# Stores of the split weights issued by ScalarE and GpSimd instead of SyncE

## The chip, the cores and the metric

The kernel runs on one core of one Trainium2 chip. The metric is the device time of one execution in microseconds; the kernel before took 3095.43 us, the median of three runs (3093.91 to 3096.95). Five engines work side by side on a core: TensorE (PE in the profile, with PEld for its weight loads), VectorE (DVE), ScalarE (ACT), GpSimd (POOL) and SyncE (SP), which computes nothing and in this kernel issues nearly all DMAs. Each engine takes its instructions in order and waits at one until its semaphores allow it.

## The reference, cut to what matters

The program computes one layer of a streaming encoder for 2048 frames of 1024 channels, in float32:

```
h = rmsnorm(x) * (1 + scale) + shift
q_lat, kv_lat, k_rope, gm_in, rw_in, z, g = split(h @ w_in)      # 7712 columns
y_mla = attention, block-causal, 8 heads; q and k,v from q_lat, kv_lat by w_uq, w_ukv
y_gm  = u * (W_s layernorm(v) + b)                               # 128-frame blocks
y_rw  = RWKV-7 recurrence: state = state * decay + ..., 8 heads of 64
merged = sum_n (y_n * silu(z_n)) @ w_br[n] * sigmoid(g_n)
out = x + gate * rmsnorm(merged @ w_out)
```

What counts here is that all 2048 frames are multiplied by the same weights `w_in`, `w_br`, `w_out`, `w_uq` and `w_ukv`, a block of frames at a time.

## The kernel before, in words

The frames are worked on in four super-blocks of 512. Within each come the projections of `w_in`, the recurrence (`wkv`), and the attention (`attention`), during which the next super-block's projections and the finishing work of the previous one fill TensorE's free time.

A product is made to near float32 accuracy from two rounded parts of each operand, a high part (the value rounded to TensorE's fast float32 format) and a low part (the rest): `mm3` multiplies high by high, high by low and low by high. A projection (`gemm`) of 128 output channels for 512 frames takes 24 such matmuls of 128 by 512, in two groups of four 128-row pieces of the weight.

`wgran` (line 558) delivers the two parts of one group's weight, 128 by 512 values, 256 KB each. When the group is asked for the first time, it loads the raw weight into a buffer `wr`, ScalarE rounds it into `wh` (the high part), and VectorE or GpSimd subtracts to make `wl` (the low part), whichever has the smaller modelled backlog (`split`, line 534). Then `keep` (line 544) stores both parts in DRAM tensors named `kept`. Every later super-block loads them from there (`again`, line 550). So the stores are issued once for each group of each weight: for `w_in` in the first super-block, for `w_br` and `w_out` a little later, up to some 1120 us. The attention's up-projection weights go the same way in tiles `wuq`, `wuqh`, `wuql` of half the size (`weights`, twelve groups). There are three buffers each of `wr`, `wh` and `wl`, and two each of `wuq`, `wuqh`, `wuql`; a buffer can be written again when all that reads it has ended, the store among them. The first super-block's output gates are projections whose 256 KB result (`gt`) is stored as well (`gate_d`).

In the recurrence each pair of heads (`hp`, four in all) makes a small triangular inverse on VectorE (`X`, `tx`), which goes to DRAM in four stores (`xd`) and comes back in another arrangement in eight loads (`xtb`) before TensorE can go on with the chain of that pair. GpSimd takes part in that chain with small operations (`el`, `bkb`, `r`, `rkb`, `m21`, `dg`, and the two operations of a reciprocal root).

The order of TensorE's instructions is written out ahead of time by a planner, `Pace`. It keeps a modelled clock: `note` (line 143) gives each instruction a duration and a place on its engine, `ready` tells when a thread of work can go on, and `run` takes the thread to be stepped next. For a DMA the clock takes 0.45 us on one place called "queue", 1.1 us of latency, the bytes' time on one place called "DMA", and 0.8 us until it is landed. The order of the other engines' instructions, SyncE's included, follows from a scheduler of the language; loads of weights are given a higher priority there, so they stand ahead of other work in SyncE's order.

Of the kernel before, what the change touches and what calls it, by code (L numbers as in the profile page):

```python
# [11 lines left out]
F32 = mybir.dt.float32  # L12
# [78 lines left out]
class Pace:  # L91
# [55 lines left out]
    def note(self, i):  # L147
        eng = str(i.engine).split(".")[-1]
        dma = "DMA" in type(i).__name__
        src, dst, n, full, f32 = [], [], 1, 0, False  # L150
        for l, aps in ((src, i.ins), (dst, i.outs)):
            for a in aps:
                ap = getattr(a, "bass_ap", None)
                if ap is None:
                    continue
                l.append(ap.tensor.name)
                m = 1
                for _, c in a.ap[1:]:
                    m *= c
                full += l is src and m > 1  # L160
                if dma:
                    m = 4 * m * a.ap[0][1]
                if eng != "PE" or l is dst:
                    n = max(n, m)
                elif a.dtype == F32:
                    f32 = True
        dep = 0.0
        for x in src:
            dep = max(dep, self.after(self.wrote.get(x), eng))
        for x in dst:  # L170
            for e in self.used.get(x, {}).items():
                if not (dma and e[0] == "DMA"):
                    dep = max(dep, self.after(e, eng))
        if eng == "PE":
            nr, nc = i.tile_size
            dur = n * (4 if f32 and not i.is_transpose else 2 if f32 else 1) / 2400 * nr * nc / P ** 2
            t = self.t = max(self.t, dep) + dur
            self.pe += dur
        elif dma:
            dur = n / 3.6e5  # L180
            t = self.slot("queue", max(dep, self.t - self.early), .45) + 1.1
            t = self.slot("DMA", t, dur) + dur + DLAT
            eng = "DMA"
        else:
            psum = any(x.startswith(("pd", "ps")) for x in src)
            op = type(i).__name__
            if eng == "Activation":
                f = str(i.func).split(".")[-1]
                if f in ("Exp", "Gelu", "Sin") and f != self.table or f == "Tanh" and self.table not in ("Exp", "Gelu"):
                    self.table = "Exp" if f == "Tanh" else f  # L190
                    t = self.slot(eng, max(dep, self.t - self.early), 1.28)
                dur = .05 + n * .00084 + .04 * (not psum) + .09 * (len(src) > 1) + .09 * (len(dst) > 1)
            elif eng == "DVE":
                dur = .065 + n / (960 if psum or full > 1 or n < 128 else 1920) + .065 * (full < len(src))
                if "Reciprocal" in op:
                    dur = .07 + n * .0063
                elif "Scan" in op or "Reduce" in op:
                    dur = n * (.0021 if "Scan" in op else .00118)
            else:
                dur = .12 + n * .00216 if n <= 512 else .55 + n * .0013  # L200
                if n <= 16 and "TensorTensor" in op:
                    dur = .3 + n * .165
            dur *= SLOW
            t = self.slot(eng, max(dep, self.t - self.early), dur) + dur
        for x in dst:

            self.wrote[x] = (eng, max(t, self.wrote[x][1]) if dma and x in self.wrote else t)
        for x in src + dst:
            u = self.used.setdefault(x, {})
            u[eng] = max(u.get(eng, 0.0), t)  # L210
# [96 lines left out]
def trunk(ctx, tc, io, out):  # L307
    nc = tc.nc
    pace = Pace()
    V, A, G, PE, SY = (pace.engine(e) for e in (nc.vector, nc.scalar, nc.gpsimd, nc.tensor, nc.sync))  # L310
# [231 lines left out]
    kept = {}  # L542

    def keep(key, h, l):

        kept[key] = [dr.tile(list(x.shape), F32, name="kept") for x in (h, l)]
        for d, x in zip(kept[key], (h, l)):
            SY.dma_start(d, x.bitcast(F32))

    def again(key, h, l):  # L550

# [6 lines left out]
    def wgran(key, fill):  # L558

        if key in kept:  # L560
            tags = [("wr", "wh"), ("wl", "wr"), ("wh", "wl")][turns[0] % 3]
            turns[0] += 1
            h, l = (wp.tile([P, 4, P], F32R, tag=g, name="wh" if n == 0 else "wl", bufs=WHB) for n, g in enumerate(tags))
            again(key, h, l)
            return h, l
        raw = wp.tile([P, 4, P], F32, tag="wr", name="wr", bufs=WRB)
        with tc.high_priority(offset=100):
            fill(raw)
        h = wp.tile([P, 4, P], F32R, tag="wh", name="wh", bufs=WHB)
        l = wp.tile([P, 4, P], F32R, tag="wl", name="wl", bufs=WHB)  # L570
        split(h, l, raw)
        keep(key, h, l)
        return h, l
# [159 lines left out]
    def mla_units(s, pl):  # L733
# [14 lines left out]
        def weights(key, fill):  # L748
            hl = wparts()
            if key in kept:  # L750
                again(key, *hl)
                return hl
            w = pl.tile([P, 2, P], F32, tag="wuq", name="wuq", bufs=2)
            fill(w)
            parts(w, *hl)
            keep(key, *hl)
            return hl
# [999 lines left out]
```

## Time and profile before

| What | us |
|---|---|
| median of three runs (lowest, highest) | 3095.43 (3093.91, 3096.95) |
| the profiled execution: its time | 3098.93 |
| its span, first to last instruction | 3096.6 |
| mean granted TensorE clock, share of full speed | 0.97 |

A page of the profile gives the busy time of each engine and its share of the span; the views behind it tell, for any stretch, what each engine waited for and what ended the wait. A row of a timeline reads: start in us from the span's start, duration in us, engine, line, operation, out<-in, shapes, count, and in brackets the engine's idle time before it with what ended that. All instructions bear line 120, a helper that records them, so one reads by the tiles' names. An engine's name with a q (SPq, ACTq) marks the sequencer's own instructions, such as the issue of a DMA, which are not counted as busy.

### The profile page before, as it was taken

What the parts mean: (1) busy time and instruction counts of PE and PEld (TensorE: products, weight loads), DVE (VectorE), ACT (ScalarE), POOL (GpSimd) and SP (SyncE); (2) the same over time, 40 slices, a digit from 0 to 9 for tenths busy, and PEclk for the clock granted to TensorE, in tenths of its full rate; (3) what the DMA queues carried; (4) which work ended last, traced back from release to release, by engine and by line L of the source; (5) the groups of instructions that cost most, each with busy time, mean ns of one, the idle gap of its engine ahead of it and who ended that gap; (6) DMA issues with size and microseconds to landing.
All of it is one profiled execution on the core that took longest, in us unless ns stands there. A gap on an engine that the chain in (4) does not pass through costs nothing.

```text
span 3096.6 us, 49478 instructions
## 1 busy us (share of the span) xinstructions
PE 2877.7 (93%) x16924; PEld 2330.6 (75%) x16924; DVE 1714.8 (55%) x4574; ACT 1235.2 (40%) x2868; POOL 598.8 (19%) x606
## 2 busy tenths in 40 slices
PE   5889988989989999999999998998899999899998
PEld 4667766777867777878877777887787677788886
DVE  6426675466257753466357653446645765356653
ACT  4325433444233433444333323454433333267641
POOL 3122232332021211131011101113100110222210
PEclk8999999989999999999999999999999999999999
DMA  7888755877766689765665578655557556844456
GB/s 270 260 273 252 223 176 164 268 237 244 231 211 196 198 252 286 223 203 173 211 210 174 167 236 266 201 164 187 160 168 243 179 158 215 263 143 134 124 183 218
DMA packets 521383, 645.84 MB, mean 209 GB/s; under 512 B 142160, under 2 KB 254892, under 8 KB 521132
## 3 DMA queue, kind: packets, MB, share of 16 engines
q1 hardware_dynamic: 520960, 642.64, 66.0%
q8 instruction: 134, 2.20, 0.3%
q14 instruction: 117, 0.96, 0.1%
q10 hardware_dynamic: 172, 0.05, 0.0%
HBM read 457.69 MB, written 184.81 MB: 207 GB/s over the span
## 4 chain that ended last, share of the span: by engine, by line
PE 59%; DVE 5%; DMA 4%; ACT 2%; issue 1%; POOL 1%; SPq 1%; POOLq 0%; DVEq 0%; ACTq 0%
PE pd L120 36%; PE pss L120 10%; PE pst L120 9%; PE pso L120 4%; DMA x<-in_x 1%; SPq L120 1%; DVE X L120 1%; DVE tx L120 0%; DMA tg<-gate_d 0%; DMA wr<-in_w_out 0%; DMA wl<-kept 0%; DMA yo<-yo_d 0%; ACT Y L120 0%; DMA xtb<-xd 0%; DMA wh<-kept 0%
## 5 line engine op out<-in xcount | busy, mean ns | idle before, releaser
L120 PE MATMUL pd<-hh,wh 128*128 128x512 f32 x1952 | 810.6, 415 | 16.7 <-ACT wh L120 6.4
L120 PE MATMUL pd<-hh,wl 128*128 128x512 f32 x1952 | 775.2, 397 | 7.8 <-POOL wl L120 5.9
L120 PE MATMUL pd<-hl,wh 128*128 128x512 f32 x1952 | 773.9, 396 | 2.8 <-DVE hl L120 1.8
L120 PEld LDWEIGHTS pd<-hh,wh 128*128 128x128 f32 x1952 | 373.3, 191 | 105.5 <-issue 13.2
L120 PEld LDWEIGHTS pd<-hh,wl 128*128 128x128 f32 x1952 | 372.2, 191 | 95.6 <-POOL wl L120 9.7
L120 PEld LDWEIGHTS pd<-hl,wh 128*128 128x128 f32 x1952 | 374.5, 192 | 71.1 <-DVE hl L120 3.6
L120 DVE TENSOR_TENSOR pw<-pst,ph 128x512 fp32r<-128x512 f32 (+2 forms) x352 | 196.3, 568 | 248.9 <-ACT ph L120 247.5
L120 ACT ACTIVATE ph<-pst 128x512 fp32r<-128x512 f32 (+2 forms) x352 | 171.5, 497 | 247.6 <-PE pst L120 211.2
L120 PE MATMUL pd<-brh,wh 128*128 128x512 f32 x576 | 252.3, 438 | 18.8 <-DVE gt L120 9.0
L120 PE MATMUL pd<-brh,wl 128*128 128x512 f32 x576 | 229.8, 399 | 0.6 <-POOL wl L120 0.6
L120 PE MATMUL pd<-brl,wh 128*128 128x512 f32 x576 | 230.2, 400 | 0.0
L120 DVE TENSOR_SCALAR_CACHE_REDUCE p<-pss 128x512 f32<-128x512 f32 (+2 forms) x320 | 191.2, 607 | 69.2 <-PE pss L120 65.2
L120 ACT ACTIVATE p<-p,nm 128x512 f32<-128x512 f32 (+3 forms) x288 | 189.7, 660 | 82.8 <-DVE nm L120 82.4
L120 POOL TENSOR_TENSOR wl<-wr,wh 128x512 fp32r<-128x512 f32 x98 | 131.2, 1341 | 435.4 <-ACT wh L120 347.5
L120 ACT ACTIVATE wh<-wr 128x512 fp32r<-128x512 f32 x162 | 101.1, 628 | 230.3 <-PE pd L120 89.0
L120 PE MATMUL pst<-consts,p 128*128 128x128 f32 x1088 | 162.4, 274 | 10.7 <-DVE za L120 5.8
L120 PE MATMUL pso<-ph,v 128*128 128x256 f32 x576 | 152.8, 288 | 0.0
L120 PEld LDWEIGHTS pd<-brh,wh 128*128 128x128 f32 x576 | 111.2, 193 | 52.3 <-issue 13.8
L120 PEld LDWEIGHTS pst<-consts,p 128*128 128x128 f32 x1088 | 128.8, 141 | 27.3 <-issue 12.0
L120 PE MATMUL pso<-pw,v 128*128 128x256 f32 x576 | 146.4, 283 | 1.2 <-DVE pw L120 1.2
L120 PE MATMUL pss<-kh,qh 96*128 96x512 f32 (+2 forms) x320 | 129.3, 404 | 18.2 <-ACT kh L120 15.2
L120 POOL TENSOR_TENSOR kl<-stg,kh 96x512 fp32r<-96x512 f32 x80 | 103.4, 1296 | 220.5 <-ACT kh L120 214.2
(295 smaller groups left out, 4820.7 us busy)
## 6 DMA issues: line engine op xcount, KB each, us to landing
wh<-kept SPq DMA_DIRECT2D x486, 256.0 KB
wl<-kept SPq DMA_DIRECT2D x486, 256.0 KB
kept<-wh SPq DMA_DIRECT2D x162, 256.0 KB
kept<-wl SPq DMA_DIRECT2D x162, 256.0 KB
wr<-in_w_in SPq DMA_DIRECT2D x120, 256.0 KB
gate_d<-gt SPq DMA_DIRECT2D x64, 256.0 KB
part_d<-gt SPq DMA_DIRECT2D x64, 256.0 KB
p<-part_d SPq DMA_DIRECT2D x64, 256.0 KB
```

Of the source, the lines that this page charges most:

```text
L120: r = f(*a, **k)
```

## The change

`keep` gives the store of the high part to ScalarE's queue (`A`) and that of the low part to GpSimd's (`G`); before, SyncE (`SY`) issued both. `keep` is called by `wgran` and by `weights`, for each group once. In the planner's clock a DMA's place on "queue" becomes a place on the queue of the engine that issues it. Buffers, tensors and bytes stay as they are, and so do the loads in `again`.

```diff
@@ -178,7 +178,7 @@
             self.pe += dur
         elif dma:
             dur = n / 3.6e5
-            t = self.slot("queue", max(dep, self.t - self.early), .45) + 1.1
+            t = self.slot("queue of " + eng, max(dep, self.t - self.early), .45) + 1.1
             t = self.slot("DMA", t, dur) + dur + DLAT
             eng = "DMA"
         else:
@@ -544,8 +544,8 @@
     def keep(key, h, l):
 
         kept[key] = [dr.tile(list(x.shape), F32, name="kept") for x in (h, l)]
-        for d, x in zip(kept[key], (h, l)):
-            SY.dma_start(d, x.bitcast(F32))
+        for e, d, x in zip((A, G), kept[key], (h, l)):
+            e.dma_start(d, x.bitcast(F32))
 
     def again(key, h, l):
```

## Rows read from the trace of the kernel before

**Rows 1.** The page: busy us of each engine, share of span, instructions.

```profile
PE 2877.7 (93%) x16924; PEld 2330.6 (75%) x16924; DVE 1714.8 (55%) x4574; ACT 1235.2 (40%) x2868; POOL 598.8 (19%) x606
```

**Rows 2.** Stretches: length, busy PE PEld DVE ACT POOL, clock, DMA share, GB/s.

```profile
0.00:30.00 30.00, 8.05 (x34) 5.45 (x34) 14.05 (x24) 16.45 (x33) 2.00 (x7) 1.00 0.91 334
88.00:126.00 38.00, 27.42 (x91) 19.48 (x90) 27.54 (x41) 10.16 (x20) 5.61 (x12) 0.82 0.81 248
130.00:242.00 112.00, 95.32 (x417) 74.18 (x418) 28.63 (x48) 32.22 (x52) 25.01 (x25) 0.97 0.84 271
242.00:640.00 398.00, 366.71 (x2334) 286.95 (x2334) 247.72 (x662) 172.88 (x369) 121.28 (x105) 0.95 0.70 218
```

**Rows 3.** Waits of PE, 126 to 242 us: total us, times, longest us.

```profile
PE pd L120 <- ACT wh L120: 6.4, 4, 2.3
PE pd L120 <- POOL wl L120: 3.6, 6, 0.9
...
PE pd L120 <- DVE wl L120: 1.6, 1, 1.6
```

**Rows 4.** Group, 130 to 242 us: busy, mean ns | idle before, what ended it.

```profile
L120 ACT ACTIVATE wh<-wr 128x512 fp32r<-128x512 f32 x30 | 18.9, 631 | 60.8 <-DMA kept<-wh 34.0 <-DMA kept<-wl 9.8 <-PE pd L120 6.0
```

**Rows 5.** ACT's timeline, 190 to 212 us.

```profile
192.97 0.63 ACT L120 ACTIVATE wh<-wr 128x512 fp32r<-128x512 f32 x1 [2.04 <-PE pd L120]
...
207.09 0.63 ACT L120 ACTIVATE wh<-wr 128x512 fp32r<-128x512 f32 x1 [0.72 <-DMA kept<-wh]
```

**Rows 6.** SP's timeline, 160 to 240 us.

```profile
203.15 0.38 SPq L120 DMA_DIRECT2D wr<-in_w_in  x1
203.59 0.50 SPq L120 DMA_DIRECT2D kept<-wh  x1
...
216.02 0.38 SPq L120 DMA_DIRECT2D wr<-in_w_in  x1
```

**Rows 7.** POOL's timeline, 190 to 212 us.

```profile
201.84 1.28 POOL L120 TENSOR_TENSOR wl<-wr,wh 128x512 fp32r<-128x512 f32 x1 [9.54 <-ACT wh L120]
```

**Rows 8.** PE's timeline, 198 to 204 us: first and last of 15 matmuls.

```profile
197.76 0.39 PE L120 MATMUL pd<-hh,wh 128*128 128x512 f32 x1
...
200.93 0.39 PE L120 MATMUL pd<-hh,wl 128*128 128x512 f32 x1
```

**Rows 9.** The tile kept, whole span, then 242 to 640 us: ns min/median/max, starts.

```profile
L120 SPq DMA_DIRECT2D kept<-wh x162: 319/446/1825, 35.0 to 1117.7; - x162
...
L120 SPq DMA_DIRECT2D kept<-wh x87: 319/444/1044, 243.1 to 638.7; - x87
```

**Rows 10.** Waits of PE, 88 to 126 us.

```profile
PE pst L120 <- DVE wuql L120: 4.2, 3, 1.9
PE pst L120 <- ACT wuqh L120: 4.0, 3, 2.1
```

**Rows 11.** SP's timeline, 90 to 96 and 460 to 470 us.

```profile
91.92 0.34 SPq L120 DMA_DIRECT2D kept<-wuql  x1
...
93.28 0.44 SPq L120 DMA_DIRECT2D wuq<-in_mla_w_uq  x1
...
462.13 0.50 SPq L120 DMA_DIRECT2D kept<-wh  x1
...
463.33 3.89 SPq L120 DMA_DIRECT2D xtb<-xd  x8
```

**Rows 12.** Waits of PE, 242 to 640 us.

```profile
PE pss L120 <- DMA xtb<-xd: 12.7, 5, 7.1
```

**Rows 13.** POOL's timeline, 284 to 316 us.

```profile
310.44 2.31 POOL L120 TENSOR_TENSOR bkb<-bk,E 128x1024 f32<-128x1024 f32 x1 [3.12 <-DMA xd<-X]
312.71 1.72 POOL L120 TENSOR_TENSOR wl<-wr,wh 128x512 fp32r<-128x512 f32 x1
```

**Rows 14.** ACT's timeline, 0 to 12 us: first and last of 11 loads.

```profile
4.68 0.25 ACTq L120 DMA_DIRECT2D rows<-in_rw_k_k  x1
...
11.12 0.30 ACTq L120 DMA_DIRECT2D rows<-in_b_ada  x1
```

## The prediction, made before the changed kernel ran

> **What bounds the kernel now.** I read the page first. TensorE is busy 2877.7 of 3096.6 us [rows 1], so at most 219 us are idle in the whole kernel, and the change can only give back idle time, or slow matmuls, in the stretches where stores of the weights' parts are issued. The table of stretches [rows 2] comes next. From 130 to 242 us, where the first projections stream their weights in, TensorE is busy 95.3 of 112 us, the DMA engines have a share of 0.84, and the granted clock is 0.97. From 242 to 640 us (the first recurrence) TensorE is busy 366.7 of 398 us, ScalarE 172.9, GpSimd 121.3.
>
> What does TensorE wait for between 126 and 242 us? Three rows name the weights' parts: 6.4 us for the high part, 3.6 and 1.6 us for the low part, 11.6 us in all [rows 3]. And what holds those parts back? The high parts are written by ScalarE, and of the 60.8 us that ScalarE idles ahead of its 30 activations, 34.0 us end with a DMA store of a high part and 9.8 us with one of a low part [rows 4]. So the three buffers of a part come free too late: a new part can't be written until the part of three groups ago is stored.
>
> One buffer followed through the timelines shows why. A high part was written at 192.97 us (0.63 us) [rows 5]. Its store was issued at 203.59 us, ten microseconds later, right behind a weight load issued at 203.15 us [rows 6]. That load waited until GpSimd had finished the low part that it began at 201.84 us (1.28 us) [rows 7], because it refills the raw buffer which that operation reads. SyncE's queue is in order, so the finished part's store sat behind a load that could not go yet. The activation that needed the buffer ran at 207.09 us, released by a store [rows 5]. This is a loop: store, buffer, part, load, next store. It turns over four groups, two gate projections, in 12.9 us (loads at 203.15 and 216.02 us [rows 6]), 6.4 us each, while TensorE's 24 matmuls of a projection need 5.4 us: 15 starts lie between 197.76 and 200.93 us, 0.226 us apart [rows 8].
>
> **The change, part by part.** It moves 162 stores of high parts [rows 9] and as many of low parts off SyncE, and 12 and 12 smaller ones of the attention's up-projections: the high parts' to ScalarE, the low parts' to GpSimd. No byte is added or removed, and no tensor changes. Of what leaves SyncE I count:
>
> First, the loop above. A high part's store no longer stands behind a load; ScalarE issues it after its own activation. At stake are the 11.6 us of rows 3. What is late next is the DMA system: 112 us at 271 GB/s become 292 GB/s if 8 us go, and the highest rate of any stretch I read is 334 GB/s at a share of 0.91 [rows 2]. I take two thirds, 8 us, between 0 and 11.6. With a clock of 0.97 the stretch also loses 0.03 x 112 = 3.4 us to slow matmuls, some of it after waits of other causes; I take 1.5, between 0 and 3.4.
>
> Second, the attention's query weights, 88 to 126 us. TensorE waits 4.2 and 4.0 us for them [rows 10]. Their raw load at 93.28 us stands behind three stores of parts that start at 91.92 us [rows 11]: 1.36 us in each of about three rounds, 4.1 us at most. I take 3. The clock there is 0.82 [rows 2], worth 6.8 us in 38; I take 1 of it, since the waits shrink and do not vanish.
>
> Third, the recurrence's way through DRAM. Ahead of the eight loads at 463.33 us stand two stores from 462.13 us on [rows 11], 1.2 us; TensorE waited 12.7 us for these loads in five waits [rows 12]. Two of the four head pairs show long waits, so 2 us, between 0 and 2.4. Sum of gains: 8 + 1.5 + 3 + 1 + 2 = 15.5 us, from 0 to 11.6 + 3.4 + 4.1 + 3 + 2.4 = 24.5.
>
> What is added. ScalarE issues 174 stores. On SyncE such an issue has a median of 0.45 us [rows 9], so about 78 us over the stretch to 1120 us. In the recurrence it is 87 stores [rows 9], 39 us, a tenth of 398 us, so each of some 80 ScalarE steps (20 for each head pair) meets one with a chance of 0.1 and waits half of 0.45: 1.8 us, half of it where TensorE hangs on the chain, 1 us. Elsewhere the second PSUM bank of the projections hides it: ScalarE's evacuation may come 5.4 us late before TensorE stops.
>
> GpSimd issuing a store is not in this trace. From below its price is SyncE's shortest issue, 0.32 us [rows 9]; from above the long GpSimd operation in the same stretch, 2.31 us [rows 13]. I take 1.3, the length of GpSimd's operation on the very same tile [rows 7]. In the recurrence as many stores, 87 x 1.3 = 113 us, bring GpSimd from 121 to 234 of 398 us [rows 2]. The code has nine GpSimd steps for each head pair (el, bkb, r, rkb, m21, two dg, two for the rsqrt), 36 in all; each finds a store ahead with a chance of 113/398 = 0.28 and waits half of 1.3 us: 6.6 us, half of it felt by TensorE, 3.3. With 0.32 us it is 0.2, with 2.31 it is 11. A low part that VectorE made adds a wait on GpSimd: behind that store stand GpSimd's next low part or its next step of the chain, and TensorE waits for either. Such a collision is to be seen already: a low part began only at 312.71 us, when the operation of 2.31 us before it was done [rows 13].
>
> Here the Trainium skill speaks against the change. SBUF — State Buffer, "Who interferes with whom", says that descriptor generation by GpSimd is blocked while VectorE works in its 2-port modes, and advises issuing from ScalarE or SyncE instead. No row here shows a store issued by GpSimd; by the rule the price would lie toward the upper end, a loss of 11 instead of 3.3 us.
>
> Third cost: ScalarE may have to wait before it may issue at all. At the start ScalarE issues eleven small loads of 0.23 to 0.31 us between 4.68 and 11.42 us [rows 14]; they fill 3 of 6.7 us, and nothing of ScalarE lies between them. The other 3.8 us, 0.38 per issue, look like waits for earlier transfers, of SyncE's too. At 0.38 x 87 = 33 us in the recurrence, worked out like the issue time, that is 0.6 us; I take 2.5, since single waits can be long, from 0 to the third rival. Sum of costs 1 + 3.3 + 2.5 = 6.8.
>
> The other edit gives the ordering clock a queue for each engine. It alters only the order of TensorE's instructions and which of VectorE and GpSimd makes a low part: with two stores in three gone from the modelled SyncE queue, loads are thought to arrive a little earlier. Before, a projection's seven DMAs took 7 x 0.45 = 3.15 us of modelled queue against 5.1 us of matmuls, so that queue seldom decided. I put this at nothing, between -10 and +10 us, roughly the largest single wait that another order could make or undo (the waits for the DRAM round trip sum to 12.7 [rows 12]).
>
> Net: 6.8 - 15.5 = -8.7 us. The profiled execution took 3098.9 us (its span 3096.6 and 2.3 us around it), which becomes 3090; it lies 3.5 us above the median of the runs, so for the median 3095.4 - 8.7 = 3087 us.
>
> **The rivals.** (1) The stores were not what mattered, and nothing measurable changes: 3095. For it: the raw loads wait for the low parts whoever stores them [rows 6, 7], and the DMA engines already have a share of 0.84. Against it: the buffer's release by a store [rows 4, 5]. The skill has this rival as a rule: DMA: Bandwidth & Descriptors, "Issuing engines are not separate DMA queues", says that several issuing engines save only the issue time. By it the time would stay; the trace disagrees so far in that the ten microseconds were an in-order wait, not issue time.
>
> (2) GpSimd becomes the bound, so the kernel is slower. In a projection GpSimd makes about one of the two low parts (1.29 us) and issues two stores; above (5.4 - 1.29) / 2 = 2.05 us for a store it can't keep up with TensorE. At 2.31 us, the first gain (8 + 1.5) is gone, 11 us are lost in the recurrence, and 3.5 us on ScalarE: 3095.4 + 11 + 3.5 - 6 = about 3104. For it: the neighbour of 2.31 us; against: GpSimd is busy only 25 of 112 us now [rows 2].
>
> (3) ScalarE stands at its stores until the eight loads of a head pair have landed. Their issue alone takes 3.89 us [rows 11], and a store issued at 203.59 us released its buffer for 207.09 us [rows 5, 6], 3.5 us later; between 3.9 and 7.4 us I estimate 6. Four head pairs make 24 us, and TensorE pays them, since ScalarE empties its banks: 3095.4 + 24 - 15.5 + 4.3 = 3108. It decides once ScalarE waits over 5.4 us, a projection's length. For it: the spread of ScalarE's own issues [rows 14]; against: in the projections, earlier transfers have landed by the time a part is made.
>
> (4) The new order decides, in either direction, by more than the stores do: 3078 or 3105.
>
> **How the numbers follow.** Forecast 0.52, rival 1 0.18, rival 2 0.08, rival 3 0.12, rival 4 0.10, half on each side. What this kernel's measurement can tell from no change is about 0.2%, 6.2 us, so 3089 to 3102 counts as the same. The forecast's own range, from its bounds, is 3071 (all gains, no cost) to 3094 (gains as taken, GpSimd at its upper price), and about a tenth of its weight lies above 3089. Faster: 0.46 + 0.05; same: 0.06 + 0.18; slower: 0.08 + 0.12 + 0.05 = 0.25. The range 3064 to 3110 takes in the full gain with a lucky order and both slower mechanisms.
>
> **What would show it.** Right: high-part stores issued within 1 us of their activation; ScalarE's activations of high parts no longer released by stores [rows 4]; the waits for parts down from 11.6 to about 4 us [rows 3]; a DMA share near 0.9 from 130 to 242 us. GpSimd's store near 1.3 us, and its busy time in the recurrence near 234 us. Wrong: stores on ScalarE that start several microseconds after the activation; more waiting for GpSimd's steps or the DRAM round trip than now [rows 12]; a first stretch as long as before. A TensorE order with many moved instructions and a changed end of the recurrence would mean rival 4.

## The result, and the profile after

The changed kernel takes 3116.41 us (median of nine runs, 3102.78 to 3132.46); the kernel before took 3095.07 us beside it (nine runs, 3089.79 to 3101.14). The ratio is 1.0069, with an interval of 1.0048 to 1.0091: slower by some 21 us, where 3087 was forecast, and outside the range of 3064 to 3110. Ratios here and below are of the runs as a whole and can differ by 0.1% from the ratio of two medians. One execution of a later experiment (high parts alone, 3796 us) is a slow one and is left out of its ratio. The profiled execution of the changed kernel took 3107.66 us, with a span of 3105.7. It lies 8.7 us below the median, so the trace shows only 9 of the 21 us as a longer span.

The page first, then the stretches (length, busy us and instructions of each engine, clock, DMA share, GB/s), against rows 1 and 2:

```profile
PE 2867.2 (92%) x16924; PEld 2327.4 (75%) x16924; DVE 1731.3 (56%) x4572; ACT 1234.8 (40%) x2870; POOL 700.3 (23%) x782
```

```profile
130.00:242.00 112.00, 108.67 (x510) 88.69 (x512) 37.49 (x67) 45.88 (x74) 55.48 (x69) 1.00 0.90 298
242.00:640.00 398.00, 343.18 (x2231) 268.65 (x2230) 249.17 (x659) 163.99 (x358) 160.23 (x184) 0.93 0.68 211
```

From 130 to 242 us the change did what it was forecast to do, and more: TensorE is busy 108.7 instead of 95.3 us, with 510 instead of 417 matmuls, at full clock, and the DMA share is 0.90. From 242 to 640 us TensorE is busy less, 343.2 instead of 366.7 us, and at 640 us the lead is gone. (This stretch ends at a fixed time and not at the same work, so it proves little: in the first experiment below, which gains, it has 354.9 us.) What TensorE waited for from 126 to 242 us is now in two rows (total us, times, longest); the waits for parts of rows 3 are gone:

```profile
PE pst L120 <- ACT vv L120: 2.2, 1, 2.2
PE pst L120 <- DVE vn L120: 1.8, 2, 1.5
```

ScalarE's group of high parts, 130 to 242 us, answers to rows 4, and its timeline to rows 5:

```profile
L120 ACT ACTIVATE wh<-wr 128x512 fp32r<-128x512 f32 x36 | 22.7, 631 | 64.7 <-PE pd L120 57.3 <-DMA wr<-in_w_in 5.3 <-DMA sg_d<-gt 2.0
```

```profile
192.13 0.63 ACT L120 ACTIVATE wh<-wr 128x512 fp32r<-128x512 f32 x1 [1.65 <-PE pd L120]
192.80 0.33 ACTq L120 DMA_DIRECT2D kept<-wh  x1
194.81 0.63 ACT L120 ACTIVATE wh<-wr 128x512 fp32r<-128x512 f32 x1 [2.04 <-PE pd L120]
```

Stores of parts are no longer among the main releasers: of the 64.7 us ahead of these activations 57.3 end with TensorE's last use of the buffer. A store is issued 0.04 us after its activation ends (192.13 + 0.63 to 192.80).

Now the stores themselves, by tile: on ScalarE and on GpSimd (ns least, median, most; first and last start), and what GpSimd's own idle time ahead of its stores was for (us, times). They answer to rows 9:

```profile
L120 ACTq DMA_DIRECT2D kept<-wh x162: 326/326/1103, 34.8 to 1108.0; - x162
```

```profile
L120 POOL DMA_DIRECT2D kept<-wl x162: 539/557/790, 36.4 to 1109.6; - x162
...
  DVE wl L120: 79.9, 33
```

A store costs GpSimd 0.56 us, not the 1.3 I had taken, but GpSimd stood 79.9 us, in 33 waits, at stores of low parts that VectorE had not made yet. That was the first suspect. The second is in the waits of TensorE from 242 to 640 us, against rows 12:

```profile
PE pss L120 <- DMA xtb<-xd: 24.9, 4, 13.3
```

The wait for the inverse's way through DRAM has doubled, and from 30 to 1140 us it is the largest of all, 42.8 us (25.2 before). TensorE's written order differs from that of before in thousands of places. So the question was whether the stores' new engines had cost the time, or the planner's new order.

### The profile page after: what moved, and what is told of

Read it like the earlier page. It is cut to its first block, busy times and chain, and to the rows that moved or that the text cites. A ratio compares the mean times of both kernels' runs of the same rounds, so it can differ in the third digit from the quotient of the medians.

```text
span 3105.7 us, 49574 instructions
## 1 busy us (share of the span) xinstructions
PE 2867.2 (92%) x16924; PEld 2327.4 (75%) x16924; DVE 1731.3 (56%) x4572; ACT 1234.8 (40%) x2870; POOL 700.3 (23%) x782
## 4 chain that ended last, share of the span: by engine, by line
PE 64%; DVE 7%; DMA 6%; issue 3%; POOL 2%; ACT 2%; SPq 2%; POOLq 0%; DVEq 0%; ACTq 0%
PE pd L120 39%; PE pss L120 11%; PE pst L120 10%; PE pso L120 4%; DMA x<-in_x 2%; SPq L120 2%; DVE X L120 1%; DVE tx L120 1%; DMA wh<-kept 1%; POOL rs L120 0%; DMA stg<-q_d 0%; DMA xtb<-xd 0%; DMA yg<-mg_d 0%; DVE Y L120 0%; DVE x L120 0%
## 5 line engine op out<-in xcount | busy, mean ns | idle before, releaser
L120 PE MATMUL pd<-hh,wh 128*128 128x512 f32 x1952 | 804.3, 412 | 11.5 <-ACT hh L120 5.5
```

What stands on the lines that cost most here:

```text
L120: r = f(*a, **k)
```

## Experiments: the stores and the order, one at a time

The planner can be told one thing and the engines given another. In the first four runs the order of TensorE is, instruction for instruction, either that of before or that of the changed kernel. The orders of the other engines follow from the scheduler and shift a little with the stores. (The clock edit alone, with the stores left on SyncE, needs no run: every engine's instructions stand in the order of before. It acts only together with the moved stores.)

**Stores moved, old order.** (The cut is against the changed kernel; the line that first sets `seen` to None and the clock's line, which is that of before, are left out here and below.)

```diff
-        eng = str(i.engine).split(".")[-1]
+        eng = self.seen or str(i.engine).split(".")[-1]
...
-        for e, d, x in zip((A, G), kept[key], (h, l)):
-            e.dma_start(d, x.bitcast(F32))
+        for e, pace.seen, d, x in zip((A, G), ("SP", "SP"), kept[key], (h, l)):
+            e.dma_start(d, x.bitcast(F32)); pace.seen = None
```

> The stores are issued by ScalarE and GpSimd as in the changed kernel, but the planner takes each for SyncE's, so TensorE's order and the choice of engine for every low part are those of the kernel before. Theory A (the new issuing engines cost the time: GpSimd stood 79.9 us at stores of low parts that VectorE had not made yet, and its steps of the recurrence came late): nearly the whole loss stays, +12 to +22 us against before (3107 to 3117), GpSimd's wait for VectorE's low parts near 80 us, and the loss lies between 242 and 1160 us. Theory B (the planner's other order of TensorE costs the time): the forecast's gain of about 9 to 13 us of the first stretch shows by itself, 3082 to 3089. If each has a share: 3095 to 3105.

Measured: 3086.57 us beside 3094.41 of before, ratio 0.9977 (0.9965 to 0.9989).

**Stores on SyncE, new order.** The reverse: the clock of the changed kernel is told ScalarE and GpSimd, while SyncE issues.

```diff
-        for e, d, x in zip((A, G), kept[key], (h, l)):
-            e.dma_start(d, x.bitcast(F32))
+        for e, pace.seen, d, x in zip((SY, SY), ("Activation", "Pool"), kept[key], (h, l)):
+            e.dma_start(d, x.bitcast(F32)); pace.seen = None
```

> The other half of the change: SyncE issues every store as before, but the planner takes them for ScalarE's and GpSimd's, with a queue each, so TensorE's order is that of the changed kernel. Theory A: near the kernel before, 3090 to 3100, with the first stretch (130 to 242 us) at TensorE 95 us busy as before. Theory B: +25 to +35 us (3120 to 3130), since it has the order's loss without the first stretch's gain. If each has a share: 3103 to 3115. If the two halves only add up, this and the run of the other half together give +21 us.

Measured: 3128.28 us, ratio 1.0114 (1.0097 to 1.0131). Theory A is out. The two ratios multiply to 1.0091, the upper end of what both halves together gave. In the old order the moved stores are worth about -7 us (-0.23% of 3094). The order costs 28 us with them (1.0069 / 0.9977 = 1.0092) and 35 us without.

Where does an order cost? Stages cut at the same landmarks: the first recurrence from its first store of `md` (an operand of the recurrence) to its last store of `yr_d` (its output), the second likewise, and then up to the third's first store of `md`. The columns are those of the stretches above. Kernel before:

```profile
266.00:581.00 315.00, 289.70 (x1936) 223.84 (x1936) 204.75 (x549) 123.15 (x251) 84.17 (x72) 0.96 0.65 200
869.00:1158.00 289.00, 266.68 (x1881) 205.44 (x1876) 187.21 (x545) 99.23 (x258) 50.10 (x46) 0.98 0.69 214
1158.00:1574.00 416.00, 406.65 (x2126) 340.19 (x2126) 202.62 (x546) 172.24 (x388) 73.87 (x77) 0.98 0.69 219
```

Stores moved, old order (ahead of the stages its stretch from 130 to 242 us):

```profile
130.00:242.00 112.00, 106.37 (x495) 86.16 (x496) 37.84 (x67) 42.43 (x71) 51.18 (x65) 0.97 0.89 291
247.00:571.00 324.00, 293.22 (x1936) 227.47 (x1934) 209.97 (x548) 123.01 (x250) 121.86 (x141) 0.94 0.63 195
862.00:1150.00 288.00, 271.04 (x1885) 208.94 (x1885) 190.40 (x547) 99.32 (x257) 61.42 (x69) 0.96 0.69 216
1150.00:1562.00 412.00, 403.49 (x2131) 337.31 (x2131) 202.98 (x548) 173.01 (x390) 73.72 (x78) 1.00 0.70 222
```

The changed kernel:

```profile
248.00:560.00 312.00, 273.47 (x1887) 211.54 (x1886) 210.46 (x545) 119.88 (x244) 117.70 (x135) 0.95 0.63 193
846.00:1152.00 306.00, 270.48 (x1880) 207.33 (x1879) 196.72 (x547) 100.92 (x261) 65.99 (x71) 0.95 0.63 200
1152.00:1591.00 439.00, 425.37 (x2199) 355.38 (x2198) 206.35 (x549) 170.88 (x390) 74.94 (x79) 0.98 0.69 219
```

Stores on SyncE, new order (the second and third of these stages):

```profile
867.00:1172.00 305.00, 271.05 (x1851) 207.18 (x1850) 192.16 (x541) 98.70 (x256) 51.91 (x48) 0.93 0.63 196
1172.00:1608.00 436.00, 421.64 (x2198) 352.40 (x2197) 206.88 (x548) 171.00 (x389) 74.74 (x78) 0.99 0.69 220
```

Length less busy time is TensorE's idle time. In the second recurrence it is 22 us before and 17 with the moved stores in the old order, but 36 and 34 us in the two kernels with the new order, whoever issues. The first recurrence of the changed kernel holds 49 matmuls fewer than in the old order (1887, 1936), of which 29 had run before it began (919 against 890 from the start of the run), and the third stage holds 68 more (2199, 2131). At the start of this stage the changed kernel is 43 matmuls behind (6034, 6077): projections that filled gaps now come later, while TensorE idled in their old place. The other 25 of the 68 stand ahead of the same landmark only in the new order. From the start of this stage to its end, the changed kernel falls from 2 us behind to 29 us behind the run with the old order (1152 to 1150, 1591 to 1562); at the end of the run it is 22 us (spans of 3105.7 and 3083.8). Of these 27 us 68 x 0.226 us [rows 8] = 15 are the matmuls at full clock; by estimate some 9 are the lower clock (0.98, 1.00), and the idle time grew from 8.5 to 13.6 us.

**High parts alone, and low parts alone**, both in the old order, by the first diff with one word changed.

```diff
-        for e, pace.seen, d, x in zip((A, G), ("SP", "SP"), kept[key], (h, l)):
+        for e, pace.seen, d, x in zip((A, SY), ("SP", "SP"), kept[key], (h, l)):
```

> Only the high parts' stores go to ScalarE, the low parts' stay on SyncE, with TensorE's order of before. Theory A, with GpSimd as the engine that costs: GpSimd waits for no low part of VectorE, so most of the first stretch's gain without the loss, 3082 to 3092. Theory A with ScalarE as the engine that costs: 3102 to 3112. Theory B: 3083 to 3092 as well, but then the run with both stores moved in the old order is at least as fast.

Measured: 3086.04 us (all eleven runs), ratio 0.9967 (0.9954 to 0.9981).

```diff
-        for e, pace.seen, d, x in zip((A, G), ("SP", "SP"), kept[key], (h, l)):
+        for e, pace.seen, d, x in zip((SY, G), ("SP", "SP"), kept[key], (h, l)):
```

> Only the low parts' stores go to GpSimd, the high parts' stay on SyncE, with TensorE's order of before. Theory A with GpSimd as the engine that costs: slower than before by 10 to 22 us (3105 to 3117), with GpSimd's wait for VectorE's low parts near 80 us. Theory A with ScalarE as the one that costs, or theory B: 3085 to 3097, since the low parts' stores still leave SyncE and GpSimd's waits are hidden.

Measured: 3093.85 us, ratio 1.0002 (0.9991 to 1.0014). The high parts' store on ScalarE brings the whole gain. Each run's first stretch and first recurrence, the high parts' run first:

```profile
130.00:242.00 112.00, 106.14 (x493) 86.05 (x492) 34.30 (x63) 39.75 (x65) 30.06 (x31) 0.98 0.92 298
254.00:571.00 317.00, 293.11 (x1938) 225.93 (x1936) 205.54 (x549) 123.38 (x251) 84.05 (x72) 0.95 0.65 200
```

```profile
130.00:242.00 112.00, 105.89 (x513) 86.23 (x511) 37.84 (x66) 42.82 (x70) 53.38 (x68) 1.00 0.89 297
248.00:579.00 331.00, 296.05 (x1933) 228.78 (x1931) 212.25 (x548) 122.35 (x250) 121.01 (x141) 0.93 0.62 191
```

Either store taken off SyncE speeds up the first projections (TensorE busy 106 of 112 us in both). With the low parts on GpSimd the recurrence then takes 331 instead of 315 us and ends at 579, where before ended at 581. (The profiled execution of this run, 3084.26 us, is its fastest, 9.6 us below the median.)

**GpSimd stores only the low parts it made.** Is it the wait for VectorE's low parts (88.2 us in the old order)?

```diff
-        e.tensor_tensor(out=lo, in0=src, in1=hi.bitcast(F32), op=ALU.subtract)
+        self_lo[0] = e; e.tensor_tensor(out=lo, in0=src, in1=hi.bitcast(F32), op=ALU.subtract)
...
-        for e, d, x in zip((A, G), kept[key], (h, l)):
+        for e, pace.seen, d, x in zip((A, G if self_lo[0] is G else SY), ("SP", "SP"), kept[key], (h, l)):
```

> TensorE's order of before, high parts' stores on ScalarE, and GpSimd stores a low part only where it made that part itself; one that VectorE made is stored by SyncE. This takes away GpSimd's waits for VectorE's low parts (88.2 us with all low parts on GpSimd in this order). If those waits cost TensorE time: faster than the run with all low parts on GpSimd (3086.6), 3075 to 3084. If they are hidden: 3083 to 3090, as that run and the one with the high parts alone.

Measured: 3091.78 us, ratio 0.9983 (0.9970 to 0.9997). GpSimd's stores and what its idle time ahead of them was for:

```profile
L120 POOL DMA_DIRECT2D kept<-wl x98: 539/557/790, 36.2 to 1107.5; - x98
...
  POOL wl L120: 27.0, 91
```

The wait for VectorE is gone and nothing was won, within some 5 us (0.9983 against 0.9977): it was hidden. The median even lies above both expected ranges. With it 64 of the low parts' stores went back to SyncE; that alone costs nothing that shows, since with all of them there the ratio is 0.9967. What lengthens the recurrence when GpSimd stores low parts is not settled by these runs; it is worth a few us at most (0.9967 against 0.9977 and 0.9983, whose intervals overlap; with the low parts' stores alone 1.0002).

## Experiments: what makes an order good

**Other orders.** Three runs change TensorE's order by what the planner's clock is told. I counted, in the written order, the projections' matmuls ahead of the second recurrence's end: 2829 of 7776 before, 2775 in the changed kernel. First, the changed kernel without its clock edit (2874):

```diff
-            t = self.slot("queue of " + eng, max(dep, self.t - self.early), .45) + 1.1
+            t = self.slot("queue", max(dep, self.t - self.early), .45) + 1.1
```

> The changed kernel without its second edit: stores on ScalarE and GpSimd, the planner knows it, but its clock keeps one queue for all DMAs. TensorE's order is then a third one, neither that of before nor that of the changed kernel. In it 2874 of the 7776 matmuls of the projections stand ahead of the end of the second recurrence, against 2829 in the order of before and 2775 in that of the changed kernel. Theory C (what the order costs goes by how many projection matmuls fill the first two recurrences): from 3086.6 with 2829 and 3116 with 2775, both with the stores moved, 0.55 us for each, so 45 more give 3062 to 3082. Theory D (any order but the tuned one is worse): 3100 to 3120. Theory E (the clock with a queue for each engine is what spoils the order): 3080 to 3095.

Measured: 3087.56 us, ratio 0.9972 (0.9956 to 0.9988). Then the changed kernel with one number altered (2862):

```diff
-            t = self.slot("queue of " + eng, max(dep, self.t - self.early), .45) + 1.1
+            t = self.slot("queue of " + eng, max(dep, self.t - self.early), .46) + 1.1
```

> The changed kernel with one number of the planner's clock altered: an issue takes 0.46 us of a modelled queue instead of 0.45. TensorE's order becomes another one, with 2862 projection matmuls ahead of the end of the second recurrence, instead of 2775. Theory C: 3116 less 30 to 48 us, so 3068 to 3086. Theory D: 3100 to 3125. Theory E (the queue for each engine spoils the order): 3105 to 3120, as the clock still has it.

Measured: 3099.70 us, ratio 1.0013 (1.0004 to 1.0023). And the kernel before, stores on SyncE, with another number (2895):

```diff
-            t = self.slot("queue", max(dep, self.t - self.early), .45) + 1.1
+            t = self.slot("queue", max(dep, self.t - self.early), .50) + 1.1
```

> The kernel before, every store on SyncE, with 0.50 instead of 0.45 us for an issue in the planner's clock. TensorE's order has 2895 projection matmuls ahead of the end of the second recurrence instead of 2829. Theory C: faster than before by 15 to 36 us, 3058 to 3080. Theory D: slower, 3100 to 3125. Theory E: no change, 3088 to 3100.

Measured: 3069.51 us, ratio 0.9915 (0.9898 to 0.9932). Theory D falls: two other orders beat that of the changed kernel, and one beats that of before by 25 us. Theory E falls too, since 0.46 in the same clock recovers 17 of the 21 us, and the last run gained 25 us where this theory expected no change. Theory C holds its range once (3058 to 3080 for the last) and misses it by 6 and 14 us in the other two: 2874 projections did no better than 2829 with the same stores (3087.56, 3086.57). A count over both recurrences says too little; it may matter in which gap a projection stands.

So I looked at the gaps. In the changed kernel, fourth head pair of the first recurrence, TensorE's timeline and SyncE's:

```profile
500.41 0.39 PE L120 MATMUL pd<-hh,wl 128*128 128x512 f32 x1
510.48 0.65 PE L120 MATMUL pss<-Pm,xtb 64*64 64x128 f32 x2 [9.68 <-DMA xtb<-xd]
```

```profile
502.76 2.58 SPq L120 DMA_DIRECT2D xd<-X  x4
...
507.23 3.71 SPq L120 DMA_DIRECT2D xtb<-xd  x8
```

While the inverse is stored and read back, 502.8 to 510.5 us, the order has no matmul for TensorE to do: it idles 9.68 us. The gap costs clock as well: the granted clock is 1.00 from 480 to 500.8 us, 0.61 in the gap to 510.4, still 0.68 from there to 520 with TensorE busy 8.8 of 9.6 us, and 1.00 again from 520 to 530. In the fourth pair of the second recurrence the same happens: 3 matmuls between store and first reader and 7.7 us idle, where the moved stores in the old order have 53 and 0.3 us. `run` lets low-ranked projections fill such gaps, up to a budget of 70 us of TensorE for a recurrence (`CAP`). Was the budget spent too early?

**A budget of 100 us.**

```diff
-CAP = [70.0, 70.0, 70.0, 100.0]
+CAP = [100.0, 100.0, 70.0, 100.0]
```

> The changed kernel with one other number in the planner: in the first two recurrences the low-ranked projections that fill gaps may take 100 us of TensorE instead of 70. TensorE's order is the same up to the second head pair; between the last matmul before the inverse and the first that reads xtb it then has 132 instead of 96 filling matmuls in the third head pair, 156 instead of 126 in the fourth, and in the fourth of the second recurrence 123 instead of 105. Theory F (the changed order costs time because the recurrences' waits for the way through DRAM lack filling work): those three waits (6.7, 7.7 and 7.7 us) mostly go, 3088 to 3098, and TensorE's wait for xtb falls from 53 to 30 to 38 us. Theory G (which order is good is not told by the filling): 3105 to 3125.

Measured: 3081.42 us, ratio 0.9962 (0.9949 to 0.9975), by the two ratios some 33 us below the changed kernel. The same head pair in this run, store at 507.86 us:

```profile
507.75 0.50 PE L120 MATMUL pd<-hh,wh 128*128 128x512 f32 x1
...
527.84 0.39 PE L120 MATMUL pd<-hh,wl 128*128 128x512 f32 x1
528.16 1.10 PE L120 MATMUL pss<-Pm,xtb 64*64 64x128 f32 x32
```

Now 91 matmuls stand between the store and the first reader, and it waits for nothing. TensorE's wait for `xtb` from 30 to 1140 us, in the changed kernel, with the old order, and with this budget:

```profile
PE pss L120 <- DMA xtb<-xd: 42.8, 8, 13.3
```

```profile
PE pss L120 <- DMA xtb<-xd: 21.7, 7, 7.1
```

```profile
PE pss L120 <- DMA xtb<-xd: 10.5, 7, 3.7
```

Theory F holds for the wait; the time fell by more than I had said (3088 to 3098). Theory C can't be told apart from it here: this order also puts 75 projection matmuls more ahead of the second recurrence's end (2850), and at 0.55 us each that is 3075.

How much of the order's cost is this wait? With the stores moved, the wait is 21.1 us longer in the new order than in the old (42.8, 21.7), as much as the two spans differ (21.9). With the stores on SyncE it is 11.5 us longer (36.7, 25.2), while the spans differ by 29.7; there the mean granted clock fell from 0.970 to 0.965, by estimate some 15 us of 3126.

**Slower engines, or a slower way through DRAM, in the planner's clock.**

```diff
-SLOW = 1.0
+SLOW = 1.1
```

> The changed kernel, and the planner's clock takes every step of VectorE, ScalarE and GpSimd for a tenth longer. More projections are then placed in the recurrences: 2970 matmuls ahead of the end of the second one, against 2775 in the changed kernel and 2895 in the fastest order run so far. Theory F: 3060 to 3085. Theory G: 3095 to 3125. By the plain count of theory C, 0.55 us each, it would be 3009; the waits left to fill (TensorE idle some 75 us in the first two recurrences of the changed kernel) don't allow it.

Measured: 3054.95 us, ratio 0.9877 (0.9858 to 0.9897).

```diff
-            t = self.slot("DMA", t, dur) + dur + DLAT
+            t = self.slot("DMA", t, dur) + dur + DLAT + 4 * any(x.startswith("xtb") for x in dst)
```

> The changed kernel, and the planner's clock takes the loads of xtb alone for 4 us longer, so it places more projections between the store of X and the first reader of xtb: 180 instead of 105 in the fourth head pair of the second recurrence, 186 instead of 138 in the second; 2976 instead of 2775 in all ahead of its end. Theory F: TensorE's wait for xtb falls from 53 us to 10 to 25, time 3070 to 3092. Theory G: the wait falls, but the chain of the recurrence comes later by as much, 3100 to 3125.

Measured: 3048.27 us, ratio 0.9857 (0.9843 to 0.9871). The wait for `xtb` from 30 to 1140 us, and the second recurrence with the stage behind it, in this last run:

```profile
PE pss L120 <- DMA xtb<-xd: 8.7, 5, 4.5
```

```profile
855.00:1168.00 313.00, 295.79 (x2021) 229.00 (x2021) 202.75 (x564) 104.88 (x267) 61.83 (x68) 0.99 0.72 229
1168.00:1543.00 375.00, 369.17 (x1977) 308.33 (x1976) 192.32 (x530) 162.23 (x375) 72.64 (x77) 1.00 0.68 215
```

The recurrence takes longer than in the changed kernel (313, 306 us), but it holds 141 matmuls more (2021, 1880), TensorE idles 17 us instead of 36, and the next stage is 64 us shorter (375, 439). Both runs are faster than theory F's ranges, by 5 and 22 us; theory G falls. Theory C's count overshoots (3009 for the first; 201 more at 0.55 us give 3006 for the second). All orders that ran with both stores moved, by matmuls ahead of the second recurrence's end:

| run | matmuls | wait for `xtb`, 30 to 1140, us | time, us |
|---|---|---|---|
| changed kernel | 2775 | 42.8 | 3116 |
| old order | 2829 | 21.7 | 3087 |
| budget of 100 | 2850 | 10.5 | 3081 |
| 0.46 us an issue | 2862 | 15.2 | 3100 |
| one queue in the clock | 2874 | 11.5 | 3088 |
| steps a tenth longer | 2970 | 8.2 | 3055 |
| 4 us more for `xtb` | 2976 | 8.7 | 3048 |

Neither column orders the times. The run with 0.46 us waits less for `xtb` than the old order and is 13 us slower; the budget of 100 waits hardly longer than the last two and takes 26 to 33 us more. Unfilled gaps are shown as a cost; a measure that prices an order is not.

**The better half of the change in a better order.** High parts on ScalarE, low parts on SyncE, TensorE's order of the kernel before at 0.50 (the planner takes each store for SyncE's, as above).

```diff
-        for e, d, x in zip((A, G), kept[key], (h, l)):
+        for e, pace.seen, d, x in zip((A, SY), ("SP", "SP"), kept[key], (h, l)):
...
-            t = self.slot("queue of " + eng, max(dep, self.t - self.early), .45) + 1.1
+            t = self.slot("queue", max(dep, self.t - self.early), .50) + 1.1
```

> High parts' stores on ScalarE, low parts' on SyncE, with the TensorE order of the kernel before at 0.50 us an issue. If the two gains add up: 3069.5 less 8 to 10, 3058 to 3063. If the better order has already hidden what the stores held up: 3066 to 3073.

Measured: 3048.67 us, ratio 0.9861 (0.9847 to 0.9876), against 0.9915 in the same order with all stores on SyncE. That is below both expected ranges (3058 to 3063, 3066 to 3073). Moving the store gains here as well (0.9861 / 0.9915 = 0.9945, 17 us); that this is more than the 10 us in the old order is not shown, as the intervals leave some 7 us either way. This version and the one with the longer way through DRAM beat the kernel before by 1.4% and the changed kernel by 2.1%.

## Why the prediction was wrong

The step that failed is the sentence on the planner: "I put this at nothing, between -10 and +10 us". The order cost 28 us. The reason I gave, that the modelled queue seldom decides, failed: 0.46 instead of 0.45 us for an issue gives another order and moved the time by 17 us. I had bounded the term by the largest single wait that another order could make; but an order makes or undoes filling in every head pair (idle time in two recurrences 74 against 48 us), and what is not filled comes back as work of its own in the next stage. Rival 4 had the mechanism, with a chance of 0.10 for both directions together; its 3105 us lies 18 us above the forecast, where the order alone cost 28. I had also put it down to the clock edit: it needs the moved stores as well, and the moved stores without it give a third order.

The rest of the sum came out near: -8.7 us forecast, -7 measured in the old order (0.9977, an interval from -11 to -3). That is in part luck, since gains and losses were both larger than forecast:

- First stretch: the waits for parts (11.6 us, of which I took 8) went altogether. So did the 8.2 us of waits for the query weights from 88 to 126 us, of which I took 3 and allowed 4.1 at most. TensorE's clock from 130 to 242 us rose from 0.97 to 1.00 in the changed kernel, but stayed at 0.97 in the old order, so the 1.5 us for it are not borne out there. The first recurrence began 19 us earlier in the old order (247 instead of 266 us) where the terms up to there sum to 13.5.
- Of these 19 us, 10 were left at the recurrence's end (571, 581). That loss of 9 us in the recurrence is more than all the costs forecast (6.8), and its cause is open; the 2 us of the way through DRAM can't be told apart.
- ScalarE's issue: 0.326 us, taken at 0.45. With the high parts alone moved the recurrence takes 317 us, where before took 315, which bears out that it costs little.
- GpSimd's issue: 0.557 us at the median and 0.790 at most, taken at 1.3; busy 160 us in the stretch of rows 2, where 234 were forecast. The wait for VectorE's low parts, which I named and did not price, was 80 to 88 us long and hidden. So GpSimd's term was made up of the wrong thing: with its stores alone moved the recurrence takes 331 us, 16 more than before, where the forecast's sum gives 0.6 us for 0.557 us an issue.

Of the rivals, the first falls: the issuing engine of the same bytes moved the time, by 7 us with both stores moved and 10 with the high parts' alone. What was won is an in-order wait: a finished part's store that stood 10 us behind a load [rows 5, 6] is now issued after 0.04 us, and the DMA rate of the first stretch rose from 271 to 298 GB/s. The Trainium skill's DMA: Bandwidth & Descriptors, "Issuing engines are not separate DMA queues", which stood behind this rival, says that issuing from several engines saves only issue time. The two timelines show more saved than that. The second falls by the 0.557 us and by GpSimd's low parts costing nothing net (1.0002). The blocking that the Trainium skill's SBUF — State Buffer, "Who interferes with whom", describes does not show in the issues, 162 of them between 539 and 790 ns; whether VectorE was in a 2-port mode beside them no row shows. The third falls by the ratio 0.9967 and by the issues on ScalarE: to 1130 us none of the changed kernel's stores starts more than 2.2 us after the instruction ahead of it (median 0.03), in the recurrences too.

Open: why the changed kernel's own runs lie so far apart (3102.78 to 3132.46), and what slows the first recurrence when GpSimd issues the low parts' stores. The first goes along with the granted clock, 0.970 in the fastest run and 0.962 in the slowest, by estimate 25 of the 30 us; why the clock differs from run to run is not shown.

## What to carry to other kernels

Where an order is written from a modelled clock, any edit that the model sees is two edits. Hold the order fixed and run the edit, then hold the edit and run the order; without that, a good change can be thrown away for a bad order. And look where an order leaves the critical chain without filling work: giving the planner a longer way through DRAM at that place took the time from 3116 to 3048 us. But run each order; neither the count of filling matmuls nor the wait left over priced the orders here.

## What was not expected of the hardware

A store of 256 KB costs its issuing engine 0.326 us on ScalarE (median of 162), 0.446 on SyncE [rows 9] and 0.557 on GpSimd, and GpSimd's never more than 0.790. I had expected GpSimd's to be some three times SyncE's.
